# Cutting the last stores of a matmul kernel differently: tiles 61 and 62 apart, the last tile whole

## The chip, the cores and the metric

The kernel runs on one core of a Trainium2 chip. The metric is the device time of one execution in microseconds (us); lower is better. The span of a profile runs from the program's first instruction to its last and is about 1.8 us shorter than the device time of the same execution (208.5 against 210.29 for the kernel before).

## The reference

```python
def setup_inputs():
    batch, m, k, n = 16, 512, 1024, 768     # x, weight, bias, residual: float32
    ...
def reference(x, weight, bias, residual):
    return (np.matmul(x, weight) + bias + residual).astype(np.float32)
```

The 16 x 512 rows are 8192 rows, or 64 tiles of 128 rows. An output tile is 128 x 768 float32, which is 384 KB.

## The kernel before

All DMA transfers are issued by SyncE (SP) in the order of one list. In it ('x', S, a, b) loads rows of x, ('r', ...) rows of the residual, ('s', S, a, b) stores finished tiles a to b-1 of group S, and ('c', 3, 15, i) stores column part i of the very last tile (63). A group has 16 tiles, so ('s', 3, 13, 15) is tiles 61 and 62.

```python
 ... ('r', 3, 7, 16), ('s', 2, 0, 16), ('s', 3, 0, 10), ('s', 3, 10, 13),
 ('s', 3, 13, 15), ('c', 3, 15, 0), ('c', 3, 15, 1)]
OUTSIDE = 4
LAST = [(0, 512), (512, 256)]
```

Row p of a tile group lies on partition p, and the tiles of one store lie side by side in a row both in SBUF and in HBM. A store of three tiles is thus 128 pieces of 9216 bytes, a store of one tile 128 pieces of 3072 bytes, and the two column parts of tile 63 are pieces of 2048 and 1024 bytes. A store is put into the program when all the tiles that it needs are finished:

```python
            if kind == "c":
                need = [("outc", j1)]                 # one column part of tile 63
            ...
            else:
                need = [("out", J * S + j) for j in range(j0, j1)]
            ...
                n0, nl = (0, N) if kind == "s" else LAST[j1]
            ...
                    dma(out_d[S, p0:p1, j0:j1, n0:n0 + nl], R[p0:p1, ..., n0:n0 + nl], ...)
```

TensorE multiplies the last tile in two column parts, and VectorE adds each part as it is finished:

```python
    for i, (n0, nl) in enumerate(LAST):
        ...                                           # 8 weight loads, 8 matmuls of nl columns
        plus("dve", row(t, n0, nl), PO[b][:, 0:nl], row(t, n0, nl), ...)
        mark("outc", i)
    mark("out", t)
```

At the end SP waits for the last four stores to land, and the program closes:

```python
        for sem, value in landed[:-OUTSIDE]:
            nc.sync.wait_ge(sem, value)
    with tc.tile_critical(sync_engine=mybir.EngineType.SP):
        for sem, value in reversed(landed[-OUTSIDE:]):
            nc.sync.wait_ge(sem, value)
```

## Time and profile before

| | before |
|---|---|
| device time, first three runs | 210.03 us median (209.96 to 210.3) |
| span of the profile | 208.5 us |
| TensorE (PE) busy | 97% |
| the sixteen DMA engines busy with queue 1 | 97.9% |
| TensorE's last matmul ends | 204.1 us |
| last store issued / landed | 204.63 / 207.27 us |

The first four rows say how long the whole takes and how full it is, the last two where the end is made. One more view of this profile is needed beside those in the prediction, SP's waits at the end (who waited for whom: us in total, times, longest us):

```profile
SPq L403 <- DMA out_dram<-ro: 1.4, 3, 0.6
```

The program waits for three separate landings after everything else is done, 1.4 us in all.

Where a single packet or a single landing is told below, it comes from the trace's packet records (start, duration, size, queue) and its semaphore events, of which each transfer has sixteen. These do not name the DMA engine, so "the late engine" is the one whose event is last of the sixteen.

### The profile page before, as it was taken

The numbers are of one execution on the slowest core, as the hardware profiler recorded it, in microseconds if no ns is written. First come the engines' busy times: TensorE is split into PE (matmuls) and PEld (weight loads), VectorE is DVE, ScalarE is ACT, GpSimd is POOL, SyncE is SP. The second block draws the span as 40 slices with busy tenths as digits, with TensorE's granted clock in tenths as the row PEclk, the third lists the DMA queues.
The fourth block names the chain that finished last, engine by engine and source line by source line (L and its number), as shares of the span: only waits on it lengthen the run. The fifth ranks groups of instructions, "written<-read, shape, count | busy, mean of one in ns | idle before, by whom it ended". The sixth has DMA issues, their size and how long they took to land.

```text
span 208.5 us, 2492 instructions
## 1 busy us (share of the span) xinstructions
PE 201.6 (97%) x1298; PEld 80.8 (39%) x794; DVE 105.3 (51%) x141; ACT 66.1 (32%) x69; POOL 115.2 (55%) x71
## 2 busy tenths in 40 slices
PE   7899999999999999999999999999999999999991
PEld 2333434443443444344334434433443443344340
DVE  1457555445545543654554454555445545544542
ACT  2444522402640282420280094230092047430000
POOL 1100029859999904999029801999207960899200
PEclk9999999999999999999999999999999999999998
DMA  5999999899999999999998999999999999999985
GB/s 216 425 425 445 426 423 475 385 427 425 485 409 416 449 395 438 453 396 437 410 493 387 432 445 429 443 443 385 423 450 468 416 398 471 415 443 417 427 351 232
DMA packets 4627, 87.20 MB, mean 418 GB/s; under 512 B 516, under 2 KB 644, under 8 KB 1416
## 3 DMA queue, kind: packets, MB, share of 16 engines
q1 hardware_dynamic: 4616, 87.05, 97.9%
q8 instruction: 8, 0.13, 0.2%
q14 instruction: 3, 0.02, 0.0%
HBM read 61.88 MB, written 25.17 MB: 417 GB/s over the span
## 4 chain that ended last, share of the span: by engine, by line
PE 92%; DMA 4%; DVE 1%; SPq 0%; ACT 0%; issue 0%
PE psum_o L257 79%; PE pt L250 13%; DMA x_tile<-in_x_dram 4%; SPq L168 0%; DVE xt L226 0%; ACT xb L226 0%; DVE ro L229 0%; SPq L403 0%; SPq L371 0%
## 5 line engine op out<-in xcount | busy, mean ns | idle before, releaser
L257 PE MATMUL psum_o<-w_sb,xt 128*128 128x256 bf16 (+1 forms) x1024 | 176.6, 326 | 0.5 <-DVE xt L226 0.5
L229 POOL TENSOR_TENSOR ro<-ro,bias_sb 128x768 f32<-128x768 f32 x50 | 88.8, 1817 | 46.9 <-DMA ro<-in_residual_dram 46.9
L226 ACT CAST xb<-x_tile 128x1024 bf16<-128x1024 f32 (+1 forms) x63 | 61.3, 1023 | 117.1 <-DMA x_tile<-in_x_dram 88.6
L268 PEld LDWEIGHTS <-xt 128*128 128x128 bf16 x520 | 50.9, 98 | 102.9 <-issue 101.0
L226 DVE COPY xt<-pt 128x1024 bf16<-128x1024 bf16 x64 | 44.1, 691 | 83.4 <-PE pt L250 83.4
L229 DVE TENSOR_TENSOR ro<-psum_o,ro 128x768 f32<-128x768 f32 (+2 forms) x51 | 47.6, 934 | 6.5 <-POOL ro L229 4.5
L250 PE MATMUL pt<-ident,xb 128*128 128x128 f32 x256 | 38.3, 274 | 0.6 <-DVE xb L226 0.4
L229 POOL TENSOR_TENSOR ro<-ro 128x768 f32<-128x768 f32 x14 | 24.9, 1818 | 25.0 <-DMA ro<-in_residual_dram 24.9
L250 PEld LDWEIGHTS pt<-ident,xb 128*128 128x128 f32 x256 | 29.7, 141 | 15.6 <-issue 12.3
L229 DVE TENSOR_TENSOR ro<-psum_o,bias_sb 128x768 f32<-128x768 f32 x14 | 13.2, 948 | 0.0
L312 PE MATMUL psum_o<-warm 128*128 128x512 bf16 x18 | 6.3, 506 | 1.4 <-DVE warm_a L232 1.4
L226 DVE CAST xb<-x_tile 128x512 bf16<-128x512 f32 (+1 forms) x4 | 1.9, 492 | 6.2 <-DMA x_tile<-in_x_dram 6.2
L226 ACT CAST w_sb<-ro 128x768 bf16<-128x768 f32 x4 | 3.3, 832 | 3.7 <-DMA ro<-in_weight_dram 3.7
L226 POOL CAST w_sb<-ro 128x768 bf16<-128x768 f32 x1 | 0.8, 822 | 6.0 <-DMA ro<-in_weight_dram 6.0
L312 PEld LDWEIGHTS psum_o<-warm 128*128 128x128 bf16 x18 | 2.1, 124 | 4.5 <-issue 2.7
L226 DVE CAST w_sb<-ro 128x768 bf16<-128x768 f32 x3 | 1.7, 557 | 2.0 <-DMA ro<-in_weight_dram 2.0
L226 ACT ACT_TABLE_LOAD x1 | 1.3, 1283 | 0.9 <-SPq L371 0.9
L329 DVE STREAM_SHUFFLE bias_sb<-bias_row 128x768 f32<-128x768 f32 x1 | 1.0, 1007 | 0.0
L232 DVE MEMSET warm<- 128x256 uint32 x1 | 0.3, 272 | 1.1 <-SPq L371 1.1
L232 DVE MEMSET bias_row<- 128x768 f32 x1 | 0.7, 698 | 0.2 <-issue 0.2
L232 POOL MEMSET ident<- 128x128 f32 x1 | 0.2, 204 | 0.5 <-SPq L371 0.5
L320 POOL TENSOR_SCALAR_AFFINE_SELECT ident<-ident 128x128 f32<-128x128 f32 x1 | 0.3, 292 | 0.2 <-POOL ident L232 0.2
(7 smaller groups left out, 0.7 us busy)
## 6 DMA issues: line engine op xcount, KB each, us to landing
out_dram<-ro SPq DMA_DIRECT2D x3, 6144.0 KB, 34.6
x_tile<-in_x_dram SPq DMA_DIRECT2D x3, 5120.0 KB, 24.5
ro<-in_residual_dram SPq DMA_DIRECT2D x3, 3840.0 KB, 32.4
x_tile<-in_x_dram SPq DMA_DIRECT2D x3, 3072.0 KB, 34.0
ro<-in_residual_dram SPq DMA_DIRECT2D x3, 2304.0 KB, 18.7
x_tile<-in_x_dram SPq DMA_DIRECT2D x4, 1024.0 KB, 10.9
x_tile<-in_x_dram SPq DMA_DIRECT2D x2, 2048.0 KB, 23.4
out_dram<-ro SPq DMA_DIRECT2D x1, 3840.0 KB, 13.3
```

What stands on the lines that cost most here:

```text
L226: op(eng, lambda e: (e.copy if eng == "act" else e.tensor_copy)(out=dst, in_=src), rd, wr)
L229: op(eng, lambda e: e.tensor_add(out=dst, in0=a, in1=b), rd, wr)
L232: op(eng, lambda e: e.memset(dst, v), [], [wr])
L250: op("pe", lambda e, q=q: e.transpose(out=pt[:, q, :], in_=words[:, ts(q, P)], identity=ident), [("XB", t % XB_N, 2 * q // n_q), "ident"], ...
L257: return e.add_instruction(mybir.InstMatmult(name=nc.get_next_instruction_name(), ins=[e.lower_ap(rhs), e.lower_ap(lhsT, for_matmul_weight ...
L268: op("pe", lambda g: g.ldweights(lhsT), rd)
L312: op("pe", lambda e: e.matmul(PO[i][:, 0:512], lhsT=warm[:, 0:P], rhs=warm, start=True, stop=True), ["warm"], [("PO", i)])
L320: op("pool", lambda e: e.affine_select(out=ident, in_=ident, compare_op=mybir.AluOpType.not_equal, fill=1.0, base=0, pattern=[[-1, P]], ch ...
L329: op("dve", lambda e: e.stream_shuffle(out=bias_sb, in_=bias_row, mask=[0] * QUAD), ["bias_row"], ["bias"])
```

## The change

The intent is to give the DMA engines tile 61 about 2 us earlier, while some of them are idle, and to replace two transfers of short pieces by one of longer pieces for the last tile.

```diff
- ('s', 3, 13, 15), ('c', 3, 15, 0), ('c', 3, 15, 1)]
+ ('s', 3, 13, 14), ('s', 3, 14, 15), ('s', 3, 15, 16)]
```

The multiplication and the addition of tile 63 keep their two column parts.

## The prediction

> **What bounds the kernel now.** I read the page first, then the chain of waits, then the timeline, the DMA issues and the stretches of the last ten microseconds, and last the trace's packet and semaphore records there. The page (engines, then queue 1, then the chain):
>
> ```profile
> PE 201.6 (97%) x1298; PEld 80.8 (39%) x794; DVE 105.3 (51%) x141; ACT 66.1 (32%) x69; POOL 115.2 (55%) x71
> ...
> q1 hardware_dynamic: 4616, 87.05, 97.9%
> ...
> PE 92%; DMA 4%; DVE 1%; SPq 0%; ACT 0%; issue 0%
> ```
>
> The reader is to see two engines at their limit at once: TensorE is busy 97% of the 208.5 us and the sixteen DMA engines 97.9%. The chain names TensorE, but that view starts from the last compute instruction and cannot see stores that end later. The change touches only stores of the last three tiles (61, 62, 63), so its worth is read after TensorE's end. The timeline of the tail (start us, duration, engine, line; the x3 group of issues is taken apart by the single windows below it, with the DMA issues of the same stores and their us to landing):
>
> ```profile
> 199.58 0.95 DVE L229 TENSOR_TENSOR ro<-psum_o,ro 128x768 f32<-128x768 f32 x1
> 201.65 0.96 DVE L229 TENSOR_TENSOR ro<-psum_o,ro 128x768 f32<-128x768 f32 x1 [1.11 <-PE psum_o L257]
> 203.30 0.69 DVE L229 TENSOR_TENSOR ro<-psum_o,ro 128x512 f32<-128x512 f32 x1 [0.70 <-PE psum_o L257]
> 204.18 0.42 DVE L229 TENSOR_TENSOR ro<-psum_o,ro 128x256 f32<-128x256 f32 x1 [0.18 <-PE psum_o L257]
> ```
>
> ```profile
> 197.52 0.33 SPq L168 DMA_DIRECT2D out_dram<-ro  x1
> 202.63 0.33 SPq L168 DMA_DIRECT2D out_dram<-ro  x1
> 204.02 0.33 SPq L168 DMA_DIRECT2D out_dram<-ro  x1
> 204.63 0.33 SPq L168 DMA_DIRECT2D out_dram<-ro  x1
> ```
>
> ```profile
> out_dram<-ro SPq DMA_DIRECT2D x1, 1152.0 KB, 6.9
> out_dram<-ro SPq DMA_DIRECT2D x1, 768.0 KB, 3.7
> out_dram<-ro SPq DMA_DIRECT2D x1, 128.0 KB, 2.6
> ```
>
> Tile 61 is finished by VectorE at 200.53 (199.58 + 0.95) and tile 62 at 202.61, yet both wait for one store issued at 202.63. Tile 63's first 512 columns are ready at 203.99 and go out at 204.02, its last 256 at 204.60 and go out at 204.63. That last store of 128 KB lands 2.6 us later, at 207.27; the span ends 1.24 us after that. How full the DMA engines are in between (stretch, its length, PE, PEld, DVE, ACT, POOL busy, clock, DMA share, GB/s):
>
> ```profile
> 198.00:202.00 4.00, 4.00 (x27) 1.61 (x17) 1.91 (x3) 0.00 (x0) 0.00 (x0) 1.00 0.89 379
> 202.00:203.50 1.50, 1.50 (x10) 0.85 (x9) 0.80 (x2) 0.00 (x0) 0.00 (x0) 1.00 0.63 264
> 203.50:206.50 3.00, 0.64 (x6) 0.32 (x4) 0.92 (x2) 0.00 (x0) 0.00 (x0) 1.00 0.96 380
> 206.50:208.50 2.00, 0.00 (x0) 0.00 (x0) 0.00 (x0) 0.00 (x0) 0.00 (x0) 0.55 0.02 6
> ```
>
> The DMA share, the last figure but one, counts: the engines idle for about a third of 202.0 to 203.5, and are full from 203.5 to the end of the data.
>
> The packet records tell which engines idle. The sixteen landings of the 1152 KB store (tiles 58 to 60) run from 202.13 to 204.44, so the engines are spread over 2.3 us: the early ones are out of work from about 201.8, the latest moves its last packet of that store at 204.09 and has the next store waiting by then. The sixteen landings of the 128 KB store are at 206.75 to 206.97 and, alone, 207.27. One late engine, never idle in the tail, sets the end.
>
> **What the Trainium skill says.** "DMA: Bandwidth & Descriptors", section "Queues, rings and completion order": a copy is split over up to sixteen rings, and each engine takes its descriptors in ring order. The trace agrees: each store has 128 packets, 8 for each engine, and an engine moves on to the next store without a gap while others are still in the last. Same page, "Why a DMA increments its semaphore by 16 and not by 1": only the full 16 means landed, each engine adding one after its own data; the trace shows 16 events for each store, so the slowest engine counts. Same page, "Anatomy of one DMA": about 2.0 us fixed, mostly write receipt, given there for transfers issued by GpSimd. Here it is less: 0.84 us from issue (202.63) to the first packet on a free engine (203.47) and 0.34 us from an engine's last packet to its landing (206.92 to 207.27), 1.2 us together. Same page, "Measured": 341 GB/s for 1 MB alone and 138 for 64 KB, which would speak against splitting. In a queue that is full the trace doesn't show that loss; see the packet times next.
>
> **The change, part by part.** All four compute engines keep exactly the same instruction order; only the three last transfers on the SP queue change, 128x1536, 128x512, 128x256 becoming three of 128x768. Their number stays three, the store count eight, and the four stores waited for last are still the last four. No issue cost is added (0.33 us each, and the issues are over 0.6 us apart).
>
> Packet cost, from start to start on one engine: 6144 B 234.5 ns, 2048 B 80 ns, 1024 B 42.4 ns. For 3072 B I have four packets of the bias load at 121 ns busy, which at the same 4 ns overlap is 117 ns; between the 2048 B and 6144 B values it would be 118.6.
>
> 1. Late engine, before: 8 x 234.5 = 1.88, plus 8 x 80 = 0.64, plus 8 x 42.4 = 0.34, sum 2.86 us after 204.09, or 206.95; the record says 206.92.
> 2. Late engine, after: tile 61 is issued at about 200.55 and its packets stand in the ring long before 204.09. Three tiles at 8 x 117 to 8 x 118.6 are 2.81 to 2.85 us. It saves 0.01 to 0.05 us: the bytes are the same and only the short packets' overhead goes.
> 3. Other engines, after: the early ones get tile 61 from 200.55 + 0.84 = 201.4 and fill their idle time with it (0.94 us). Tile 62 comes at 203.47 and takes them to about 204.4; engines with a mid place (204.19 landing, so data until 203.85) are done with both at 205.7. Tile 63, issued at 204.63 as a whole, starts at 205.47 on a free engine and ends at 206.4, landing 206.75. That is 0.5 us before the late engine, and about level with their present landings of 206.75 to 206.97.
>
> Sum: the end moves from 207.27 to about 207.24; span 208.5, time 210.0 where it was 210.03.
>
> **Rivals.** A: the last transfer sets the end. At 204.63 it grows from 128 KB to 384 KB, and if the queue were empty that adds 8 x 117 - 8 x 42.4 = 0.6 us, a time of 210.6. For it speaks that nothing of tile 63 leaves before 204.63; against it, that its present 2.6 us to landing is mostly waiting behind other packets on the ring (an empty engine would take 0.84 + 0.34 + 0.34 = 1.5 us), and the larger store on an empty engine takes 2.1, still less. B: the idle time is won. Mean idleness in 202.0 to 203.5 is 0.37 x 1.5 = 0.55 us an engine, and with all of it saved the time would be 209.5. For it speaks that the engines are full afterwards; against it, that the idle engines are not the late one, and that tile 63 cannot arrive before 205.47 for anybody, which alone caps the gain at 207.27 - 206.75 = 0.5 us. C: with fewer engines active at once the late one speeds up. Packets of 6144 B stretch to 244 to 266 ns around 205.0 on the early engines, so there is contention, but the late engine's stay at 234; I give it 0.1 us at most.
>
> **Range and chances.** My main case is 0 to 0.05 us faster, with B and C as parts on one side (down to 209.5) and A as a part on the other (up to 210.6), neither likely whole. The three runs of before span 209.96 to 210.3, so the spread of a median of three is about 0.1 to 0.2 us by itself. I take 209.65 to 210.35 around 210.0. Two per cent are 4.2 us, more than all that comes after TensorE's end at 204.1 could plausibly give up or add, so same is nearly sure.
>
> **What would show it.** Right: stores of 384 KB issued near 200.55, 202.63 and 204.63; DMA share well above 0.63 in 202.0 to 203.5 and lower after 203.5; packets of 3072 B about 121 ns; the last landing within 0.15 us of 207.27 and set by one late engine. Wrong: the last store's sixteen landings bunched (then the issue of tile 63 sets the end, A or B), or the late engine gone or later by half a microsecond for a reason that the stores don't tell, or any shift before 200 us, where nothing was changed.

## The result, and the profile after

The changed kernel takes 210.18 us (median of 6 runs, 209.91 to 210.31), the kernel before 210.00 (6 runs, 209.96 to 210.38). The ratio is 1.0003, with a 95% interval of 0.999 to 1.0016: the same time. Ratios are computed as the mean time of one kernel's runs over that of the other's in the same rounds, so they are not quite the ratio of the medians quoted.

The page of the changed kernel (engines, queue 1, chain):

```profile
PE 200.5 (96%) x1273; PEld 80.9 (39%) x794; DVE 105.5 (51%) x141; ACT 66.1 (32%) x69; POOL 115.2 (55%) x71
...
q1 hardware_dynamic: 4616, 87.05, 98.0%
...
PE 88%; DMA 7%; SPq 2%; issue 1%; ACT 0%; DVE 0%; ACTq 0%
```

Both engines at the limit are as they were. (25 matmul records are missing in this trace, x1273 where x1298 were; the program has the same number.) The timeline of SP's issues, and the DMA issues of the first and the last of them with their us to landing:

```profile
200.51 0.33 SPq L168 DMA_DIRECT2D out_dram<-ro  x1
202.59 0.33 SPq L168 DMA_DIRECT2D out_dram<-ro  x1
204.58 0.33 SPq L168 DMA_DIRECT2D out_dram<-ro  x1
```

```profile
out_dram<-ro SPq DMA_DIRECT2D x1, 384.0 KB, 4.5
out_dram<-ro SPq DMA_DIRECT2D x1, 384.0 KB, 2.3
```

Tile 61 leaves at 200.51, where it waited until 202.63 before. It takes 4.5 us to land since it stands in each engine's queue behind the store of tiles 58 to 60. The same stretches as in the prediction (the last two figures are the DMA share and GB/s):

```profile
198.00:202.00 4.00, 4.00 (x28) 1.63 (x17) 1.96 (x3) 0.00 (x0) 0.00 (x0) 1.00 0.89 379
202.00:203.50 1.50, 1.50 (x11) 0.87 (x10) 0.73 (x2) 0.00 (x0) 0.00 (x0) 1.00 0.82 340
203.50:206.50 3.00, 0.59 (x6) 0.29 (x3) 0.94 (x2) 0.00 (x0) 0.00 (x0) 1.00 0.79 316
206.50:208.50 2.00, 0.00 (x0) 0.00 (x0) 0.00 (x0) 0.00 (x0) 0.00 (x0) 0.75 0.00 0
```

The idle time of 202.0 to 203.5 was filled (share 0.63 before, 0.82 now: 0.29 us for each engine), and idle time appeared after 203.5 (0.96 before, 0.79 now: 0.51 us). The work was moved, not shortened; the rest of the difference is a smaller backlog in this execution, as the next lines show. At the end SP now waits for one landing:

```profile
SPq L403 <- DMA out_dram<-ro: 0.9, 1, 0.9
```

The wait is 0.5 us shorter than before, and this execution's span is 208.1 us against 208.5. That difference is not the change: the profiled execution is the fastest of the six (209.91 us), and the spans of the other five are 208.3 to 208.5. The store of tiles 58 to 60, which no edit touched, already finished 0.37 us earlier in this trace (204.07 against 204.44).

### The profile page after: what moved, and what is told of

Same layout as the page of the kernel before. It is cut to its first block, busy times and chain, and to the rows that moved or that the text cites. A ratio compares the mean times of both kernels' runs of the same rounds, so it can differ in the third digit from the quotient of the medians.

```text
span 208.1 us, 2467 instructions
## 1 busy us (share of the span) xinstructions
PE 200.5 (96%) x1273; PEld 80.9 (39%) x794; DVE 105.5 (51%) x141; ACT 66.1 (32%) x69; POOL 115.2 (55%) x71
## 4 chain that ended last, share of the span: by engine, by line
PE 88%; DMA 7%; SPq 2%; issue 1%; ACT 0%; DVE 0%; ACTq 0%
PE psum_o L257 76%; PE pt L250 13%; DMA x_tile<-in_x_dram 7%; SPq L168 2%; ACT xb L226 0%; DVE ro L229 0%; SPq L403 0%; ACTq L104 0%; SPq L371 0%
```

## The experiments

My theory before the experiments had two arms. One arm is the issue of the last store: its packets begin about 0.84 us after it and its landing follows. The other is the backlog of the DMA engine that is furthest behind. The later arm sets the last landing, and the program ends a fixed time after it. Rival A takes the first arm alone, rival B counts bytes alone. The table sums up what the profiles showed; the third and fourth columns are the first and the last of the sixteen landings of the last store.

| kernel | last store issued | first landing | last landing | span |
|---|---|---|---|---|
| before | 204.63 | 206.75 | 207.27 | 208.5 |
| changed | 204.58 | 206.71 | 206.88 | 208.1 |
| after_again | 204.91 | 207.03 | 207.41 | 208.7 |
| split_only | 204.97 | 206.63 | 207.49 | 208.7 |
| merge_only | 204.47 | 206.64 | 206.91 | 208.2 |
| one_store | 204.68 | 208.65 | 208.83 | 210.1 |
| after_light | 204.58 | 206.73 | 206.89 | 208.1 |
| before_light | 204.42 | 206.56 | 206.72 | 208.0 |
| split_light | 204.73 | 206.40 | 206.58 | 207.8 |
| half_pe | 195.43 | 204.94 | 207.30 | 208.5 |
| no_pe | 196.11 | 204.83 | 207.03 | 208.3 |
| more_fetch | 205.25 | 207.39 | 207.66 | 208.9 |

In all twelve the span is the last landing plus 1.24 us. So the last landing is all that has to be explained.

### split_only: the first half of the change

```diff
- ('s', 3, 13, 15), ('c', 3, 15, 0), ('c', 3, 15, 1)]
+ ('s', 3, 13, 14), ('s', 3, 14, 15), ('c', 3, 15, 0), ('c', 3, 15, 1)]
```

> Half the change: tiles 61 and 62 in their own stores, tile 63 still as 512 and 256 columns. My theory (the last engine to finish is behind by its own backlog, which no cut of the stores changes): last landing still 206.9 to 207.3, time 210.0 to 210.2, ratio to before 0.999 to 1.001; the sixteen landings of the last store spread again, the late one alone at the end, with the early ones at about 206.2 (issue 204.6 + 0.84 + 8 x 42 ns + 0.34). Rival A (the moment at which the last store is issued and its size set the end): 0.5 us faster than the changed kernel, 209.6, all sixteen landings at about 206.2.

Measured: 210.26 us (5 runs), the kernel before 210.21 (11 runs), ratio 0.9998 (0.9986 to 1.001). Fifteen landings run from 206.63 to 207.36, and one comes at 207.49; the spread is 0.85 us. The last landing lies 0.19 us above the 206.9 to 207.3 that I had expected, in a profile that fell on the slowest of the five runs. The first landing, expected at about 206.2, missed by more: the last store was issued 0.37 us later than I had taken, and its packets began 0.96 us after that, behind those of the 512-column store. Rival A, which needed 209.6, falls.

### merge_only: the second half

```diff
- ('s', 3, 13, 15), ('c', 3, 15, 0), ('c', 3, 15, 1)]
+ ('s', 3, 13, 15), ('s', 3, 15, 16)]
```

> The other half: tiles 61 and 62 in one store, tile 63 in one. My theory: same bytes on the late engine, time 210.0 to 210.2, ratio 0.999 to 1.001; early engines land at about 206.75 (204.6 + 0.84 + 8 x 117 ns + 0.34). Rival A would have this the slowest of the cuts, 0.6 us over before, 210.6.

Measured: 210.19 us, ratio 0.9997 (0.9985 to 1.0009). Rival A, which needed 210.6, falls here too. Neither half does anything that can be seen by itself in the full kernel, beyond the quarter of a microsecond that the interval leaves.

### one_store: all three tiles in one store

```diff
- ('s', 3, 13, 15), ('c', 3, 15, 0), ('c', 3, 15, 1)]
+ ('s', 3, 13, 16)]
```

> Tiles 61, 62 and 63 in a single store, issued when tile 63 is done at 204.6: the engines now do run empty, the late one too (it ends the store of tiles 58 to 60 at 203.7 to 204.1). My theory: first packets at 205.45, 8 packets of 9216 B at 344 ns are 2.75 us, receipt 0.34, so all landings at 208.5 to 208.7, which is 1.3 to 1.6 us after those of before: time 211.4 to 211.8. Rival B (bytes alone count, the queue is fed early enough): 210.0.

Measured: 211.85 us (211.77 to 211.96), ratio 1.0077 (1.0065 to 1.0089), the one cut that costs time. The issue of the last store with its us to landing, and two stretches of its tail:

```profile
204.68 0.33 SPq L168 DMA_DIRECT2D out_dram<-ro  x1
```

```profile
out_dram<-ro SPq DMA_DIRECT2D x1, 1152.0 KB, 4.2
```

```profile
203.50:206.50 3.00, 0.69 (x7) 0.37 (x4) 0.97 (x2) 0.00 (x0) 0.00 (x0) 1.00 0.36 151
206.50:208.50 2.00, 0.00 (x0) 0.00 (x0) 0.00 (x0) 0.00 (x0) 0.00 (x0) 0.70 0.90 369
```

The DMA engines have run dry: their share is 0.36 from 203.5 to 206.5, where before it was 0.96. Now even the late engine waits for the issue, and the sixteen landings are within 0.19 us. Rival B falls: the same bytes cost 1.6 us more when they are handed over after the queue has emptied. The last landing is 0.1 us above the range expected and the median 0.05 us; the packets of this store took 354 ns where 344 were taken, and the engines do not all start at once.

### after_again: the changed kernel, unaltered

> The changed kernel unaltered, for noise and for the state of its tail in a second profile. My theory: time 209.9 to 210.3, ratio 0.999 to 1.001; last landing anywhere from 206.75 (all engines together, as in its first profile) to 207.3 (one late engine alone, as in the profile of before). If the last landing were again all sixteen engines within 0.2 us, the change would have moved the end from the late engine to the issue of tile 63.

Measured: 210.13 us (6 runs), ratio 1.0 (0.9987 to 1.0012). Its profile fell on a slower execution, 210.43 us. The last DMA issue and a stretch:

```profile
out_dram<-ro SPq DMA_DIRECT2D x1, 384.0 KB, 2.5
```

```profile
202.00:203.50 1.50, 1.50 (x10) 0.69 (x8) 0.89 (x1) 0.00 (x0) 0.00 (x0) 1.00 0.90 375
206.50:208.50 2.00, 0.00 (x0) 0.00 (x0) 0.00 (x0) 0.00 (x0) 0.00 (x0) 1.00 0.13 49
```

Data still moves after 206.5, and the landings run to 207.41 with a spread of 0.38 us: here the late engines are behind the issue arm again. In the changed kernel's first profile the two arms met: that spread was 0.17 us. The same program thus ends by either arm, from one execution to the next.

### after_light, before_light, split_light: no backlog

In three kernels the store of tiles 58 to 60 is left out. Their outputs are wrong, which doesn't matter for the times.

```diff
 # after_light
- ('r', 3, 7, 16), ('s', 2, 0, 16), ('s', 3, 0, 10), ('s', 3, 10, 13),
+ ('r', 3, 7, 16), ('s', 2, 0, 16), ('s', 3, 0, 10),
  ('s', 3, 13, 14), ('s', 3, 14, 15), ('s', 3, 15, 16)]
 # before_light: the same cut, with  ('s', 3, 13, 15), ('c', 3, 15, 0), ('c', 3, 15, 1)
 # split_light:  the same cut, with  ('s', 3, 13, 14), ('s', 3, 14, 15), ('c', 3, 15, 0), ('c', 3, 15, 1)
```

> The changed kernel without the store of tiles 58 to 60 (1152 KB, 2.75 us of each engine's queue; the result is wrong on purpose in those rows). The late engine then has no backlog when the last stores come. My theory: all sixteen landings of the last store within 0.2 us, 2.1 to 2.2 us after its issue (0.84 + 0.94 + 0.34), near 206.75; time 209.6 to 209.9, 0.2 to 0.4 us under before. Rival (the late engine never mattered, the issue of tile 63 set the end all along): same as the changed kernel within 0.1.

> The kernel before without the store of tiles 58 to 60 (wrong on purpose there). My theory: tiles 61 and 62 in one store occupy every engine from issue + 0.84 for 8 x 234 ns, then the two column stores follow in the queue without a pause, so the last landing is at 206.7 to 206.8 as well: within 0.1 us of the light changed kernel, 209.6 to 209.9. Rival A alone (the smaller last store lands 0.6 us earlier): 209.1 to 209.3.

> Tiles 61 and 62 apart and tile 63 in its two column stores, without the store of tiles 58 to 60 (wrong on purpose there). With no backlog and an early tile 61 the last store of 128 KB meets engines that are free or nearly so. My theory: last landing 1.5 to 1.6 us after its issue, near 206.2, time 209.1 to 209.4, 0.5 us under the light changed kernel: so the cost of merging the last tile is real, and was hidden behind the late engine in the full kernels. If it equals the light changed kernel, that cost does not exist.

Measured: after_light 209.85 us, before_light 209.90, split_light 209.61, and the kernel before in the same rounds 210.14. The ratios to before are 0.9987 (0.9975 to 1.0), 0.9987 (0.9975 to 1.0) and 0.9971 (0.9957 to 0.9984). The first two intervals just reach 1. The means of the five runs are 209.90, 209.90 and 209.57.

In all three the landings of the last store lie within 0.20 us: with the backlog gone the late engine has disappeared. The cut of before and the changed one end at the same time, as the second expectation said. Only split_light is faster than these two, by 0.33 us on the means (95% interval about 0.06 to 0.6, worked out from the runs listed). Its last issue with its us to landing:

```profile
out_dram<-ro SPq DMA_DIRECT2D x1, 128.0 KB, 1.9
```

From last issue to last landing it takes 1.85 us, after_light 2.31 (206.89 - 204.58; 2.1 to 2.2 were expected). So the cost of sending the last tile whole is real, 0.46 us in these profiles, and so is the gain of splitting tiles 61 and 62. The kernel before has neither the cost nor the gain, the changed kernel has both. My range for split_light (209.1 to 209.4) was missed by 0.2 us: the packets of the 256-column store began 0.97 us after its issue, since they stood behind those of the 512-column store, and they took 48 ns each.

### half_pe: nearly half of TensorE's work left out

```diff
+        half = HEAD <= t < n_t - 1
+        if half and e == 1:
+            return
         op("pe", lambda g: g.ldweights(lhsT), rd)
...
-                  q == 0 and e == 0, q == n_q - 1 and e == 1,
+                  q == 0 and e == 0, q == n_q - 1 and (e == 1 or half),
```

> The changed kernel with every second weight load and its two matmuls left out for tiles 3 to 62 (wrong on purpose): TensorE's work falls by nearly half and the bytes stay. If the DMA queue is what the whole kernel waits for: TensorE's share falls from 97% to about 60%, and the time stays within 1 us of before, 209.2 to 210.2, with the last store's landings spread by the lateness that the engines have gathered. If TensorE is the bound, as the chain of waits names it: the time falls by tens of us.

Measured: 210.35 us (5 runs), ratio 1.0008 (0.9995 to 1.002). The engines and queue 1 in its page:

```profile
PE 139.7 (67%) x803; PEld 63.0 (30%) x554; DVE 105.2 (50%) x141; ACT 66.0 (32%) x69; POOL 115.0 (55%) x71
...
q1 hardware_dynamic: 4616, 87.05, 97.8%
```

TensorE's busy time falls by 62 us and the time does not fall. (TensorE's share is 67% where about 60% was expected, at a granted clock of 0.87, and the time is 0.15 us above the expected range.) The last store is issued at 195.43, nine microseconds earlier than in the changed kernel, and still lands from 204.94 to 207.30. So the work of the DMA queue fills the whole time by itself, and TensorE is not the only bound. The chain of waits, which gave TensorE 92%, showed what is linked without a gap, not what sets the time. TensorE is a second bound close behind, though: the light kernels take about 2.75 us of work from every DMA engine and gain only 0.26 us, since the last store, which waits for TensorE's end, is issued no earlier (204.58 in after_light and in the changed kernel).

### no_pe and more_fetch: why is one engine late?

In the profile of before the engines land within 0.50 us of each other up to 23.15 us. A 16 KB packet of the instruction queue (queue 8) starts at 23.84. At the next landing one engine is 1.3 us behind all others (28.64 and 29.96 are the last two). Later packets of this kind, some 24 us apart, are followed by more late engines. This agrees with the Trainium skill, "Runtime: NRT & Kernel Launch", section "Terms", which says that an engine's instruction memory is refilled in 16 KiB blocks: 8 such packets are in each profile with the full TensorE program and 5 in half_pe. I formed the theory that serving such a packet makes an engine late, and took the packets away by leaving TensorE almost no program:

```diff
-            for q in range(n_q):
+            for q in range(0 if HEAD <= t < n_t - 1 else n_q):      # transposes
...
+        few = HEAD <= t < n_t - 1
+        if few:
+            return                                                   # weight loads and matmuls
```

> The changed kernel with no TensorE instruction at all for tiles 3 to 62 (wrong on purpose); bytes, stores and their cut unchanged. In all profiles so far the engines land together within 0.5 us until a 16 KB instruction packet of queue 8 appears near 24 us; from the next landings on, one engine is 1.3 us behind, and there are 8 such packets with the full TensorE program and 5 with half of it. My theory: the late engines are those that served such a packet. Then with next to no TensorE program there are 0 or 1 such packets; with none, the landings stay within 0.5 to 0.9 us to the end and the last one comes at 204.3 to 205.5, time 207.5 to 208.8, 1.3 to 2.5 us under before; with one, that engine alone stays 1.3 us behind and the gain is about half. Rival (the lateness comes from the data transfers themselves or from the chip): spread 2.0 to 2.4 us as before and 210.0 to 210.4, as with half the TensorE program.

Measured: 210.08 us, ratio 0.9995 (0.9983 to 1.0008). The engines and the queues in its page:

```profile
PE 22.1 (11%) x98; PEld 8.7 (4%) x74; DVE 104.0 (50%) x141; ACT 64.3 (31%) x69; POOL 114.7 (55%) x71
...
q1 hardware_dynamic: 4616, 87.05, 97.8%
q14 instruction: 3, 0.02, 0.0%
```

No packet of queue 8 is left, and half of the theory holds. The middle of the sixteen landings of the 3840 KB store comes at 199.64 us instead of 200.86 in the changed kernel, so most engines are indeed 1.2 us less behind. The half that counts falls, though: one engine is still 1.4 us behind the second last at the end (207.03 and 205.65), and the time is as before. It lost 0.7 us after an 8 KB instruction packet of queue 14 at 36.33, and 0.8 us more between the landings at 70.80 and 80.92, where no instruction packet is on record. In that stretch all twelve profiles show the same thing: between 75 and 79 us, 6 to 26 data packets of 30720 B, of many engines, take over 150 ns longer than the usual 1138, up to 1.2 us longer. The changed kernel's first profile has the mildest case (6 packets, at most 0.32 us longer) and is its fastest run; split_only and after_again have severe ones (over 1.1 us) and end late. That is a hint and no more: no_pe has one of 1.19 us and its last landing is at 207.03. What this disturbance is, the profiles do not tell.

The other direction adds instructions to ScalarE:

```diff
         cast(t + 2)
+        for _ in range(8):
+            copy("act", warm_a, warm_a, ["warm_a"], ["warm_a"])
```

> The changed kernel with 8 tiny copies (1x2) on ScalarE after each cast, some 480 instructions more (result correct, ScalarE busy about 160 us of 208 and still no bound). My theory: ScalarE's longer program brings 1 to 4 more instruction packets, and the last landing comes later when one of them falls on an engine that is already late: 0 to 1.3 us, time 210.0 to 211.5, with more engines in the late group in the middle of the kernel. Rival (instruction packets do not make engines late): 210.0 to 210.3 and the same grouping.

Measured: 210.65 us (210.63 to 210.79), ratio 1.0023 (1.0009 to 1.0037), result correct. The engines and the instruction queues:

```profile
PE 202.4 (97%) x1298; PEld 80.9 (39%) x794; DVE 105.3 (50%) x141; ACT 152.0 (73%) x557; POOL 115.2 (55%) x71
...
q8 instruction: 8, 0.13, 0.2%
q14 instruction: 6, 0.05, 0.1%
```

Three more packets of queue 14 came, and after the one at 161.68 us the last engine falls from 2.35 to 2.80 us behind the first. But the end did not follow that engine. The last store was issued at 205.25, 0.67 us later than in the changed kernel's first profile; its sixteen landings lie within 0.27 us, and the first comes 2.14 us after the issue, as it did there (2.13). So it followed the issue. TensorE waited 0.44 us at 171.57 for a cast of ScalarE, a wait that the changed kernel's first profile doesn't have after 140 us; so the added copies themselves are the likelier cause, which no run tests apart. This one shows that more packets came, and neither supports nor refutes that they move the end.

No cut that was tried beats both kernels with a correct result. The one that ends earliest without a backlog, split_only, is worth nothing while the backlog is there.

## Why the prediction was right

The time and the range held: 210.0 predicted within 209.65 to 210.35, 210.18 measured.

- Step 1, the late engine before: its sum reproduces the record and was not disputed by any run. That a full DMA queue holds the end where it is, with TensorE done nine microseconds earlier, is now shown by half_pe.
- Step 2, the same bytes for the late engine: the packets of 3072 B took 122 ns on average in the changed kernel, 121 were taken. Its saving of 0.01 to 0.05 us lies below what the interval of 0.13% (0.27 us) can show; the times neither confirm nor refute it. The landings do better: from its landing in the store of tiles 58 to 60 to its last one, the last engine takes 2.83 us in before (204.44 to 207.27), and with the changed cut 2.78 in after_again (204.63 to 207.41), 2.78 in half_pe and 2.77 in no_pe. That is 0.05 us, if the last of the sixteen is the same engine each time. (The bandwidths that the prediction quotes from the section "Measured" are given there for loads into SBUF issued from GpSimd, not for stores issued by SP.)
- Step 3, the other engines: they land from 206.71 on, where 206.75 was worked out. What was mis-sized is the stagger between them, which the step left out: on free engines (after_light) the last of the sixteen lands 0.16 us after the first. The "0.5 us before the late engine" is a property of one execution, not of the kernel. In the changed kernel's first profile the margin was gone, in after_again the spread was 0.38 us.
- The sum, a last landing at 207.24: the two profiles of the changed kernel have 206.88 and 207.41. The lateness of the engines before the change acts scatters by more than the change could move, and I had taken the kernel before's single profile as its typical one. The other arm scatters too: in the nine profiles with TensorE's and ScalarE's programs unaltered the last store is issued from 204.42 to 204.97. So the hit on the time is a weak test: the cuts of split_only and merge_only would have hit it as well.
- The sign that I had named as wrong, the sixteen landings bunched, did occur in the first profile. It means that the issue of tile 63 had just caught up with the backlog in that execution. The time stays the same, since both arms end within 0.5 us of each other. The other sign of being wrong, a shift before 200 us, occurred as well: the store that was issued at 158.0 landed at 192.15, against 192.60 before. In after_again, the same program, it landed at 192.85, so this is scatter and not the change.
- Rivals A and B, in the prediction's sense (the larger last store costs, the filled idle time gains), were both parts of the truth, as the light kernels show: sending the last tile whole costs 0.46 us and the earlier tile 61 wins it back. Each is visible only when no engine has a backlog. Rival C, a faster late engine, was not separated from the scatter by any run.

The filled stretch (0.63 to 0.82), the idle stretch after it (0.96 to 0.79) and the issue times (within 0.05 us of those named) came as predicted.

## What to carry to other kernels

When the DMA queue has work from start to end, as here, the cut of the last stores moves idle time about and not the end, as long as the queue does not run dry: keep it fed. The spread of the sixteen landings alone doesn't tell whether it ran dry (0.17 us in the changed kernel's first profile, 0.19 in one_store, which takes 1.6 us longer); the busy share of the tail, 0.79 against 0.36 from 203.5 to 206.5, does. A chain of waits that names a compute engine for 92% of the span does not prove that engine to be the only bound. Leave the work of each suspect out in turn and time the wrong result: here leaving out nearly half of TensorE's work gained nothing and leaving out 2.75 us of the queue's gained 0.26 us, since the other bound stood close behind. Before you read a few tenths of a microsecond from two profiles, look at spots that the change can't have touched, and at how typical each profiled run is.

## What the Trainium skill lacked or had wrong

- "DMA: Bandwidth & Descriptors", "Anatomy of one DMA", gives about 2.0 us fixed cost, for transfers issued by GpSimd. For a store issued by SP onto free engines these runs show 1.2 us: 0.83 to 0.84 us from issue to first packet and 0.34 us from an engine's last packet to its landing. So the receipt, to which that section gives most of its 2.0 us, is here the smaller part.
- No page that I read says what an instruction packet costs the data on its engine: one packet of 16 KB takes 0.9 to 1.1 us here, and the first of them is followed by one engine that is 1.3 us behind. In no_pe, without these packets, most engines are 1.2 us less behind at the end.
- "CRC Debugging", section "Comparing the Two Runs", places instruction refills on queue 14. Here the blocks of 16 KB are on queue 8 (8 of them), and three of 8 KB within the kernel are on queue 14.
- No page that I read has the disturbance between 75 and 79 us: 6 to 26 packets in each of twelve profiles over 150 ns longer than usual, up to 1.2 us, whatever the kernel.
